# One 512-column matmul for both parts of x in the convolved projection, and a later place for the scan's scaled blocks

## The chip, the cores and the metric

The kernel runs on one core of a Trainium2 chip. The metric is the device time of one execution in microseconds (us); of several runs the median is taken. Five engines work side by side, each in the order of its own queue: TensorE (PE: matmuls; PEld: its weight loads), VectorE (DVE), ScalarE (ACT), GpSimd (POOL) and SyncE (SP), which issues the loads. Tiles in SBUF and accumulators in PSUM (eight banks of 512 float32 columns) pass between them behind semaphores.

## The reference

One layer of a hybrid encoder, 256 tokens (`SEQ`), 2048 features, all float32. What matters here is the first sub-layer:

```python
hn = rmsnorm(h, mix_norm_pre[i])
proj = hn @ w_in[i]                                   # 2048 x 3616
z, xbc, dt_raw, u = jnp.split(proj, split_at, axis=-1)
y_ssd = ssd_mixer(z, xbc, dt_raw, ...)                # below
y_pool = pool_mixer(u, pool_w[i], pool_scale[i])
mix = jnp.concatenate([y_ssd, y_pool], axis=-1) @ w_out[i]
...
def ssd_mixer(z, xbc, dt_raw, conv_w, conv_b, ...):
    xbc = jax.nn.silu(dwconv_centred(xbc, conv_w, conv_b))   # 5 taps along the tokens, 1536 channels
    xs, bm, cm = jnp.split(xbc, [D_SSD, D_SSD + G * SSD_STATE], axis=-1)
    dt = jax.nn.softplus(dt_raw + dt_bias)
    # forward and backward scan in chunks of 128 tokens:
    #   y_diag = (cm bm^T) * decay * dt  @ xs     within a chunk
    #   y_off  = what the other chunk's state adds
    y = (y_fwd + y_bwd + xs * d_skip) * silu(z)
    return group_rmsnorm(y) * norm_w
```

After it come a gated conv-MLP (`w_ffn_up`, `w_ffn_down`) and a gated embedding (`w_ple_gate`, `w_ple`). Their code is not touched.

## The kernel before

Matmuls are made in a rounded float32 format. To keep the accuracy, every operand is split into a high part (rounded by ScalarE, `split` line 152, `put` line 196) and a low part (the rest, VectorE, lines 153 and 197), and a product is the sum of three: high × high, high weights × low x, low weights × high x. Weights arrive by SP in `raw` tiles of 2048 columns (4 buffers) and are split into `whi` and `wlo` tiles of 1024 columns (5 buffers each).

Nothing in the program fixes the order across engines except the order in which it is written (a planner takes what is ready by that order, on times that it estimates, and hands out buffers as they come free) and `issue_after`, which puts an instruction behind another on its engine. The planned order of each engine's queue is then fixed.

The stages at the front, one after another on TensorE: `dtu` (dt and the pool mixer's input, six PSUM buffers), the convolved projection `xbc` in three slabs of 512 features (slab 2, then 0, then 1), and z. PSUM has six `main` buffers of one bank and two `misc` ones.

A slab (`xbc`, line 672) is computed with features on the partitions by `feature_major` (line 300): four units `u`, each of one raw tile (4 blocks of 128 rows of the weights × 512 features), split into two tiles `j`; in a tile two blocks `kk` of rows, each with four blocks `f` of 128 features. For one (`kk`, `f`) the three products are three matmuls of 256 columns (the tokens). `acc` has two main buffers, with two `f` in each. The last unit runs by `f`, so that the first sums are done sooner. `times_rows` (line 426) multiplies the sums from PSUM by the tokens' norm `rxb`, 512 columns at a time. `conv` (line 434) then makes four ScalarE products and 16 VectorE steps, and line 680 finishes the SiLU.

`hn` is a `Panel`: the high parts of x for eight blocks of rows in one page, the low parts in another. `Pairs` (line 180), which the later stage `ga`/`va` uses with `feature_pairs`, keeps high and low parts of a block side by side, so that `both(k)` is one operand of 512 columns; there the sum of the low half is added to the high half at the end by `total` (line 357: a ScalarE copy from PSUM and a VectorE add).

Between units `aside()` runs the next list of jobs in `work`: for the scan `seg` (decays `E`), `cb`, `scale_by_dt` (line 685: eight ScalarE products of a block by dt into a page `w`), `weigh` (line 693: two VectorE operations of 1024 columns on `w` and `E`), `xs_turn`, `far` and `skip` (POOL products), `mix` (the scan's matmuls `yo`, `yd`). The lists stand by slab and by z's eight units (two blocks `k` of 1024 columns each, matmuls of 512 columns in four main buffers).

Of the kernel before, what the change touches and what calls it, by code (L numbers as in the profile page):

```python
# [14 lines left out]
ALU = mybir.AluOpType  # L15

P = 128
L = 256
D = 2048
NK = D // P  # L20
# [31 lines left out]
def build(nc, a, out):  # L52
# [5 lines left out]
    with tile.TileContext(nc) as tc, \  # L58
# [15 lines left out]
        def mid(name, dtype=F32):  # L74
            return gp.tile([P, 1024], dtype, tag="mid", bufs=5, name=name)
# [10 lines left out]
        def mm(o, lhsT, rhs, start, stop):  # L86
            last["pe"] = ins(nc.tensor.matmul(o, lhsT, rhs, start=start, stop=stop, skip_group_check=True))  # L87
# [53 lines left out]
        def parts(name):  # L141

            if name in spare:
                return spare.pop(name)
            return [wp.tile([P, 1088], F32R, tag=tag, bufs=5, name=f"{name}{tag}") for tag in ("whi", "wlo")]

        def split(dst, src, c0, *cuts):

            hi, lo = dst
            for c1 in cuts:  # L150
                s = slice(c0, c1)
                last["act"] = ins(nc.scalar.copy(hi[:, s], src[:, s]))
                last["dve"] = ins(nc.vector.tensor_sub(lo[:, s], src[:, s], hi[:, s].bitcast(F32)))  # L153
                c0 = c1
            return hi, lo
# [144 lines left out]
        def feature_major(name, w, c0, get, acc):  # L300

            for u in range(4):
                r = raw(f"{name}r{u}", w[u * 512:(u + 1) * 512, c0:c0 + 512]
                        .rearrange("(k p) c -> p k c", p=P), 4, 512)
                tiles = []

                def step(j, kk, f):
                    k = 4 * u + 2 * j + kk
                    (wh, wl), (xh, xl) = tiles[j], get(k)
                    s = slice(kk * 512 + f * P, kk * 512 + (f + 1) * P)  # L310
                    for q, (ww, xx) in enumerate(((wh, xh), (wh, xl), (wl, xh))):
                        mm(acc[f // 2][:, f % 2 * L:(f % 2 + 1) * L], ww[:, s], xx,
                           k == 0 and q == 0 and f % 2 == 0, k == NK - 1 and q == 2)

                for j in range(2):
                    tiles.append(split(parts(f"{name}{u}_{j}"), r[:, j * 1024:(j + 1) * 1024], 0, 1024))
                    if u < 3:
                        for kk in range(2):
                            for f in range(4):
                                step(j, kk, f)  # L320
                if u == 3:
                    for f in range(4):
                        for j in range(2):
                            for kk in range(2):
                                step(j, kk, f)
                aside()

        def feature_pairs(name, w, c0, get, acc):
# [27 lines left out]

        def total(o, acc):

            for f in range(2):
                nc.scalar.copy(o[:, f * L:(f + 1) * L], acc[f][:, L:])  # L360
                nc.vector.tensor_add(o[:, f * L:(f + 1) * L], o[:, f * L:(f + 1) * L], acc[f][:, :L])

# [60 lines left out]
            nc.vector.tensor_add(o4[:, :, :L - 1], o4[:, :, :L - 1], b4[:, :, 1:])  # L423
            return o

        def times_rows(name, acc, rb):
            o = mid(name)
            for i in range(2):
                nc.vector.tensor_tensor(o[:, i * 512:(i + 1) * 512].rearrange("p (f t) -> p f t", f=2),
                                        acc[i].rearrange("p (f t) -> p f t", f=2),  # L430
                                        rb.unsqueeze(1).to_broadcast([P, 2, L]), op=ALU.mult)
            return o

        def conv(name, acc, taps, wcol, wstep, bcol):

            cv = mid(name)
# [11 lines left out]
            return cv  # L448


        hn = Panel("hn")

        def x_panel(k0, k1):
            for k in range(k0, k1):
# [215 lines left out]
                nc.scalar.activation(xs[:, t * 1024 + slab * 512:t * 1024 + (slab + 1) * 512], ps, AF.Copy, scale=0.5)  # L670

        def xbc(slab):
            acc = main(f"xbc{slab}")
            feature_major(f"xb{slab}", w_in, DSSD + slab * 512, hn, acc)
            sc = times_rows(f"xr{slab}", acc, rxb)
            cv = conv(f"cv{slab}", sc, 5, V_SCW + 4 * slab, 12, V_SCB + 4 * slab)
            th = mid(f"th{slab}")
            nc.scalar.activation(th, cv, AF.Tanh, scale=0.5)

            nc.vector.scalar_tensor_tensor(cv, th, 1.0, cv, op0=ALU.add, op1=ALU.mult)  # L680
            return cv
# [47 lines left out]
        def job(f, *args):  # L729
# [15 lines left out]
        ])  # L745
        xa = xbc(0)
        work.extend([
            [job(seg, 3), job(scale_by_dt, 0, 0, 0)],
            [job(seg, 4), job(scale_by_dt, 0, 0, 1), job(weigh, 0, 0)],
            [job(seg, 5), job(xs_turn, xa, 0)],  # L750
            [job(seg, 6)],
        ])
# [14 lines left out]
        zacc = [main(f"z{t}") for t in range(2)]  # L767
# [382 lines left out]
```

## Time and profile before

| | |
|---|---|
| median of 3 runs | 1118.17 us (1117.62 to 1120.74) |
| the profiled execution | 1116.37 us, of which the span from first to last instruction 1114.6 |
| granted TensorE clock | 0.998 |
| busy: PE, DVE, ACT, POOL | 1102.6, 834.2, 683.7, 53.0 us |
| matmuls of the three slabs | from 52.4 to about 139.8 us, 576 of them |
| z | from 140.3 to about 195 us |
| DMA queue q1 | 274.33 MB, 73.3% of 16 engines' span |

The page of the profile gives busy times by engine, the chain of work that ended last, and the costliest groups of instructions, each named by the tiles that it writes and reads (`xbc<-hnh,xb_0whi` is a matmul into `xbc` from the high part of x and the high weights of a slab's even tile). In the views that follow, an instruction row is: start, length, engine, line, operation, names, shapes, and in brackets the idle time ahead of it with what ended it. A matmul's row is longer than its share of the pipeline; the pitch from start to start is what it costs. A slab is shown under one name (`xbc`), all its tiles under `xb_0`, `xb_1`.

### The profile page before, as it was taken

How to read it: one execution, taken by the hardware profiler on the slowest of the kernel's cores; microseconds unless marked ns; L12 is line 12 of the kernel's file. 1: busy time of each engine (PE TensorE's matmuls, PEld its weight loads, DVE VectorE, ACT ScalarE, POOL GpSimd, SP SyncE). 2: the span in 40 equal slices, each digit the busy share in tenths (PEclk: the TensorE clock that was granted, in tenths of full speed). 3: DMA queues.
4: the chain of work that ended last, by engine and by line, in shares of the span. 5: the costliest groups of instructions: out<-in, count | busy, mean ns of one | idle time of the engine just before them, and what ended most of it. 6: DMA issues, size and time to landing. Idle time of an engine off the chain costs nothing.

```text
span 1114.6 us, 15714 instructions
## 1 busy us (share of the span) xinstructions
PE 1102.6 (99%) x6040; PEld 964.0 (86%) x6040; DVE 834.2 (75%) x1047; ACT 683.7 (61%) x1006; POOL 53.0 (5%) x80
## 2 busy tenths in 40 slices
PE   9999999999999999999999999999999999999996
PEld 9999988888788888888888888888888888887885
DVE  6668888879786866767767777676888787897574
ACT  6757876555775565565655655556666466657462
POOL 0300023100200000000000000000000000001001
PEclk9999999999999999999999999999999999999999
DMA  9954445766587977877887797676888789886732
GB/s 354 375 175 150 154 151 186 262 215 224 213 283 252 302 264 247 272 268 255 270 296 254 241 323 255 211 254 205 279 293 303 255 285 314 307 283 214 247 132 76
DMA packets 145739, 275.69 MB, mean 247 GB/s; under 512 B 5504, under 2 KB 98560, under 8 KB 142208
## 3 DMA queue, kind: packets, MB, share of 16 engines
q1 hardware_dynamic: 145376, 274.33, 73.3%
q8 instruction: 47, 0.77, 0.3%
q10 hardware_dynamic: 288, 0.36, 0.1%
q14 instruction: 28, 0.23, 0.1%
HBM read 251.86 MB, written 22.81 MB: 246 GB/s over the span
## 4 chain that ended last, share of the span: by engine, by line
PE 92%; DMA 3%; ACT 2%; issue 1%; DVE 1%; POOL 0%; SPq 0%; DVEq 0%; POOLq 0%; ACTq 0%
PE va L87 22%; PE ga L87 21%; PE dna L87 15%; PE gt L87 7%; PE woa L87 7%; PE xbc L87 6%; PE dns L87 5%; PE z L87 4%; DMA dtur<-w_in 2%; DMA x<-x 1%; PE wos L87 1%; PE yd L87 1%; PE pw L87 1%; PE ple L87 0%; PE seg L87 0%
## 5 line engine op out<-in xcount | busy, mean ns | idle before, releaser
L87 PE MATMUL ga<-wox,ug_0whi 128*128 128x512 f32 x352 | 87.8, 391 | 0.0
L87 PE MATMUL va<-wox,uv_0whi 128*128 128x512 f32 x352 | 87.6, 391 | 0.0
L87 PE MATMUL ga<-wox,ug_1whi 128*128 128x512 f32 x352 | 87.2, 389 | 0.0
L87 PE MATMUL va<-wox,uv_1whi 128*128 128x512 f32 x352 | 86.9, 389 | 0.0
L87 PEld LDWEIGHTS va<-wox,uv_1whi 128*128 128x128 f32 x352 | 66.1, 188 | 13.7
L87 PEld LDWEIGHTS ga<-wox,ug_1whi 128*128 128x128 f32 x352 | 66.0, 188 | 13.7
L87 PEld LDWEIGHTS va<-wox,uv_0whi 128*128 128x128 f32 x352 | 64.6, 188 | 12.5
L87 PEld LDWEIGHTS ga<-wox,ug_0whi 128*128 128x128 f32 x352 | 64.6, 188 | 12.4
L87 PE MATMUL ga<-wox,ug_1wlo 128*128 128x256 f32 x352 | 49.7, 283 | 0.9 <-DVE ug_1wlo L153 0.9
L87 PE MATMUL ga<-wox,ug_0wlo 128*128 128x256 f32 x352 | 49.5, 283 | 0.0
L87 PE MATMUL va<-wox,uv_1wlo 128*128 128x256 f32 x352 | 49.4, 283 | 0.0
L87 PE MATMUL va<-wox,uv_0wlo 128*128 128x256 f32 x352 | 49.2, 283 | 0.0
L87 PEld LDWEIGHTS ga<-wox,ug_0wlo 128*128 128x128 f32 x352 | 46.8, 191 | 1.8
L87 PEld LDWEIGHTS va<-wox,uv_0wlo 128*128 128x128 f32 x352 | 46.7, 191 | 1.7
L87 PEld LDWEIGHTS ga<-wox,ug_1wlo 128*128 128x128 f32 x352 | 45.4, 192 | 1.3 <-DVE ug_1wlo L153 1.3
L87 PEld LDWEIGHTS va<-wox,uv_1wlo 128*128 128x128 f32 x352 | 45.4, 192 | 0.0
L875 POOL TENSOR_SCALAR dnm<-dnq,fmean 128x1 f32<-128x1 f32 x2 | 0.6, 282 | 586.8 <-ACT dnj L872 586.8
L87 PE MATMUL xbc<-hnh,xb_0whi 128*128 128x256 f32 x96 | 27.6, 288 | 0.3 <-ACT u L539 0.3
L87 PE MATMUL xbc<-hnh,xb_1whi 128*128 128x256 f32 x96 | 27.3, 285 | 0.0
L87 PE MATMUL xbc<-hnl,xb_1whi 128*128 128x256 f32 x96 | 27.2, 283 | 0.0
L87 PE MATMUL xbc<-hnh,xb_1wlo 128*128 128x256 f32 x96 | 27.1, 283 | 0.0
L87 PE MATMUL xbc<-hnh,xb_0wlo 128*128 128x256 f32 x96 | 27.1, 283 | 0.0
(1664 smaller groups left out, 3095.6 us busy)
## 6 DMA issues: line engine op xcount, KB each, us to landing
dn0r<-w_ffn_down SPq DMA_DIRECT2D x15, 1024.0 KB, 6.2
dn1r<-w_ffn_down SPq DMA_DIRECT2D x15, 1024.0 KB, 6.9
br<-w_ffn_down SPq DMA_DIRECT2D x14, 1024.0 KB, 5.5
bm<-block SPq DMA_DIRECT2D x14, 1024.0 KB, 5.0
zr<-w_in SPq DMA_DIRECT2D x8, 1024.0 KB, 5.3
wo0r<-w_out SPq DMA_DIRECT2D x8, 1024.0 KB, 5.8
gt0r<-w_ple_gate SPq DMA_DIRECT2D x8, 1024.0 KB, 5.9
gt1r<-w_ple_gate SPq DMA_DIRECT2D x8, 1024.0 KB, 5.5
```

The source lines that it names most:

```text
L87: last["pe"] = ins(nc.tensor.matmul(o, lhsT, rhs, start=start, stop=stop, skip_group_check=True))
L875: nc.gpsimd.tensor_scalar(m, q, 1.0 / D, mean[t], op0=ALU.mult, op1=ALU.add)
```

## The change

Three things are done together. First, `hn` becomes `Pairs`, and `feature_major` makes of the first two of the three products one matmul of 512 columns (high weights × both parts of x) into a bank of its own, the third a 256-column matmul into that bank's second half; a slab has four main buffers (`xbc` and `xbd`). Second, the order in a unit: both tiles are split first; in units 1 and 2 all 16 high or all 16 low matmuls run together (unit 1 low first, unit 2 high first); units 0 and 3 go by `f`, four high and four low matmuls for each. The sums are then made by `total` (four copies and four adds of 256 columns) and one multiplication by `rxb` over 1024 columns. Third, `scale_by_dt` and `weigh` leave slab 1 and stand a unit or two later in z's list.

```diff
             for u in range(4):
                 r = raw(f"{name}r{u}", ...)
-                tiles = []
-                def step(j, kk, f):
...
-                    for q, (ww, xx) in enumerate(((wh, xh), (wh, xl), (wl, xh))):
-                        mm(acc[f // 2][:, f % 2 * L:(f % 2 + 1) * L], ww[:, s], xx,
-                           k == 0 and q == 0 and f % 2 == 0, k == NK - 1 and q == 2)
...
+                r = r[:, :1024], r[:, 1024:]
+                tiles = [split(parts(f"{name}{u}_{j}"), r[j], 0, 1024) for j in range(2)]
+
+                def step(low, j, kk, f):
                     k = 4 * u + 2 * j + kk
+                    ww = tiles[j][low][:, kk * 512 + f * P:kk * 512 + (f + 1) * P]
+                    if low:
+                        mm(acc[f][:, L:], ww, get(k)[0], False, False)
+                    else:
+                        mm(acc[f], ww, get.both(k), k == 0, False)
+
+                steps = [(j, kk, f) for j in range(2) for kk in range(2) for f in range(4)]
+                if u in (0, 3):
+                    steps.sort(key=lambda x: x[2])
+                n = 4 if u in (0, 3) else 16
+                for q in range(0, 16, n):
+                    for low in (1, 0) if u and (u + q // 4) % 2 else (0, 1):
+                        for x in steps[q:q + n]:
+                            step(low, *x)
                 aside()
...
-        hn = Panel("hn")
+        hn = Pairs("hn")
...
         def xbc(slab):
-            acc = main(f"xbc{slab}")
+            acc = main(f"xbc{slab}") + main(f"xbd{slab}")
             feature_major(f"xb{slab}", w_in, DSSD + slab * 512, hn, acc)
-            sc = times_rows(f"xr{slab}", acc, rxb)
+            sc = mid(f"xr{slab}")
+            total(sc, acc)
+            s4 = sc.rearrange("p (f t) -> p f t", f=4)
+            nc.vector.tensor_tensor(s4, s4, rxb.unsqueeze(1).to_broadcast([P, 4, L]), op=ALU.mult)
...
-            [job(seg, 3), job(scale_by_dt, 0, 0, 0)],
-            [job(seg, 4), job(scale_by_dt, 0, 0, 1), job(weigh, 0, 0)],
+            [job(seg, 3)],
+            [job(seg, 4)],
             [job(seg, 5), job(xs_turn, xa, 0)],
             [job(seg, 6)],
...
-            [job(seg, 7), job(scale_by_dt, 0, 1, 0)],
-            [job(scale_by_dt, 0, 1, 1), job(weigh, 0, 1)],
-            [job(xs_turn, xb, 1), job(far, 1), job(skip, 0), job(scale_by_dt, 1, 0, 0)],
-            [job(far, 0), job(skip, 1), job(scale_by_dt, 1, 0, 1), job(weigh, 1, 0)],
-            [job(mix, 0, 0), job(scale_by_dt, 1, 1, 0)],
-            [job(mix, 0, 1), job(scale_by_dt, 1, 1, 1), job(weigh, 1, 1)],
-            [job(mix, 1, 0)],
+            [job(seg, 7)],
+            [job(scale_by_dt, 0, 0, 0), job(scale_by_dt, 0, 0, 1)],
+            [job(xs_turn, xb, 1), job(far, 1), job(skip, 0), job(weigh, 0, 0), job(scale_by_dt, 0, 1, 0)],
+            [job(scale_by_dt, 0, 1, 1), job(weigh, 0, 1), job(far, 0), job(skip, 1), job(scale_by_dt, 1, 0, 0)],
+            [job(mix, 0, 0), job(scale_by_dt, 1, 0, 1), job(weigh, 1, 0)],
+            [job(mix, 0, 1), job(scale_by_dt, 1, 1, 0), job(scale_by_dt, 1, 1, 1)],
+            [job(mix, 1, 0), job(weigh, 1, 1)],
             [job(mix, 1, 1)],
```

`total` now runs over all buffers that it is given (`len(acc)`) and `times_rows` is gone.

More of the change, by code (lines that the diff above doesn't have):

```diff
@@ L304, in feature_major @@
                         .rearrange("(k p) c -> p k c", p=P), 4, 512)
-                tiles = []
-                def step(j, kk, f):
+                r = r[:, :1024], r[:, 1024:]
+                tiles = [split(parts(f"{name}{u}_{j}"), r[j], 0, 1024) for j in range(2)]
+                def step(low, j, kk, f):
                     k = 4 * u + 2 * j + kk
-                    (wh, wl), (xh, xl) = tiles[j], get(k)
-                    s = slice(kk * 512 + f * P, kk * 512 + (f + 1) * P)
-                    for q, (ww, xx) in enumerate(((wh, xh), (wh, xl), (wl, xh))):
-                        mm(acc[f // 2][:, f % 2 * L:(f % 2 + 1) * L], ww[:, s], xx,
-                           k == 0 and q == 0 and f % 2 == 0, k == NK - 1 and q == 2)
[L315 to L325, printed above, removed]
+                    ww = tiles[j][low][:, kk * 512 + f * P:kk * 512 + (f + 1) * P]
[11 more added lines that the diff above has]
+                            step(low, *x)
                 aside()
@@ L357, in total @@
         def total(o, acc):
-            for f in range(2):
+            for f in range(len(acc)):
                 nc.scalar.copy(o[:, f * L:(f + 1) * L], acc[f][:, L:])
@@ L424, in taps @@
             return o
[L426 to L432, printed above, removed]
         def conv(name, acc, taps, wcol, wstep, bcol):
```

## Prediction

> **What bounds the kernel now.** I read the page first, its busy times and its chain, then the chain of waits piece by piece over the stage that changes, then who waited for whom there, then the time lines of VectorE and ScalarE.
>
> ```profile
> span 1114.6 us, 15714 instructions
> PE 1102.6 (99%) x6040; PEld 964.0 (86%) x6040; DVE 834.2 (75%) x1047; ACT 683.7 (61%) x1006; POOL 53.0 (5%) x80
> PE 92%; DMA 3%; ACT 2%; issue 1%; DVE 1%; POOL 0%; SPq 0%; DVEq 0%; POOLq 0%; ACTq 0%
> ...
> PE xbc L87 <- ACT u L539: 0.3, 1, 0.3
> ```
>
> The last row is the only wait that the view of waits gives for PE from 48 to 200 us, which holds the whole changed stage: the three slabs of the convolved projection (in the order 2, 0, 1) and z. TensorE is the bound there. A microsecond taken from its stream is a microsecond of the kernel, as long as no new wait opens; other engines matter through the leads that they have on it.
>
> **The matmuls.** All 576 matmuls of the projection have 256 columns. These are pieces of the chain of waits (start, length, what; the last slab ends where the `seg` row begins, and the `yd` row is used further down):
>
> ```profile
> 93.79 5.76 PE xbc L87 x48
> 120.36 5.74 PE xbc L87 x48
> 139.81 0.47 PE seg L87 x2
> 140.28 5.45 PE z L87 x24
> 193.42 1.73 PE yd L87 x16
> 338.31 22.23 PE ga L87 x128
> ```
>
> 48 narrow ones take 5.74 to 5.76 us: 119.7 ns each, 359 ns for the three of one block. The later stage `ga` already does what the change does here (one 512-column matmul for both parts of x, one of 256 for the low weights): 128 in 22.23 us, 347.3 ns a pair. z's 24 matmuls of 512 columns give 227 ns each, and 347 − 120 agrees. After the change the 192 blocks have 384 matmuls: 192 × (359 − 347) = 2.3 us saved (2.2 to 2.4 with the two readings of a unit), all on the path.
>
> The Trainium skill, "TensorE: Matmul & The Clock Gate", section "Back-to-back issue gap", gives a warm gap of N/2.4 + 2.5 ns. By that rule the block falls from 327.5 to 325 ns, an estimate of 0.5 us in all. The trace does not agree: 119.7 and 227 ns carry some 13 ns above N/2.4, so the measured saving is the larger one.
>
> **The start.** The first slab takes the buffers of the `dtu` sums; its second buffer came late:
>
> ```profile
> 52.41 0.36 PE L87 MATMUL xbc<-hnh,xb_0whi 128*128 128x256 f32 x1
> 53.09 0.28 PE L87 MATMUL xbc<-hnh,xb_0wlo 128*128 128x256 f32 x1
> 53.69 0.39 PE L87 MATMUL xbc<-hnh,xb_0whi 128*128 128x256 f32 x1 [0.32 <-ACT u L539]
> 53.11 0.53 ACT L539 ACTIVATE u<-dtu,rx0r 128x320 f32<-128x320 f32 x1 [1.65 <-DVE dt L538]
> 54.89 0.55 ACT L542 ACTIVATE u<-dtu,rx1r 128x352 f32<-128x352 f32 x1
> 51.69 1.22 DVE L153 TENSOR_TENSOR xb_1wlo<-xb2r,xb_1whi 128x1024 fp32r<-128x1024 f32 x1
> ```
>
> From 53.09 to 53.69 is 0.6 us where 0.12 is the pitch: 0.48 us lost. The new order does all of f = 0 first (8 matmuls, 4 × 347 = 1.39 us), so the second buffer is wanted at 53.8, after the 53.64 at which ScalarE is done; the third and fourth at 55.2 and 56.6, against 55.44 for the last of the `dtu` evictions. It asks for the second low tile at 53.5, ready at 52.91. So 0.5 us more is gained, with 0 as the other end.
>
> **What is added.** Leaving PSUM was one multiplication per two blocks; now it is copy, add, multiply.
>
> ```profile
> L360 ACT COPY gr<-ga x44: 372/378/382, 308.0 to 760.7; 128x256 f32<-128x256 f32 x44
> L361 DVE TENSOR_TENSOR gr<-gr,ga x44: 411/414/416, 308.8 to 761.5; 128x256 f32<-128x256 f32 x44
> L429 DVE TENSOR_TENSOR xr<-xbc,rxb x6: 682/688/693, 79.4 to 140.1; 128x512 f32<-128x512 f32 x6
> L680 DVE SCALAR_TENSOR_TENSOR cv<-th,cv x3: 1206/1215/1217, 97.0 to 150.1; 128x1024 f32<-128x1024 f32 x3
> L690 ACT ACTIVATE w<-cbm,dt x64: 385/390/405, 110.3 to 173.4; 128x128 f32<-128x128 f32 x64
> L696 DVE TENSOR_TENSOR w<-w x4: 1208/1217/1882, 122.0 to 174.9; 128x1024 f32<-128x1024 f32 x4
> L698 DVE TENSOR_TENSOR E<-E,w x4: 1206/1214/1225, 123.5 to 177.2; 128x1024 f32<-128x1024 f32 x4
> L446 DVE SCALAR_TENSOR_TENSOR cv<-xr,vt,cv x48: 465/476/484, 86.1 to 147.9; 128x254 f32<-128x254 f32 x24, 128x255 f32<-128x255 f32 x24
> ```
>
> Per slab ScalarE gets four copies (1.5 us) and VectorE four adds and a 1024-wide multiply, priced by the row of that width (4 × 0.414 + 1.215), less two at 0.688: +1.5 us. Nothing goes to POOL or SP. On the path this costs nothing as long as the weight tiles still come ahead of TensorE. The work is hidden by this slack:
>
> ```profile
> 86.00:106.00 20.00, 20.00 (x165) 19.87 (x165) 20.00 (x34) 14.58 (x23) 0.00 (x0) 1.00 0.37 115
> 113.00:126.00 13.00, 13.00 (x107) 12.82 (x106) 12.93 (x24) 12.14 (x23) 0.00 (x0) 1.00 0.25 83
> 140.00:153.00 13.00, 13.00 (x60) 10.74 (x59) 13.00 (x22) 11.71 (x21) 0.00 (x0) 1.00 0.25 81
> 153.00:166.00 13.00, 13.00 (x61) 10.76 (x61) 8.27 (x8) 7.58 (x15) 6.43 (x3) 1.00 0.69 244
> ```
>
> Columns: length, then busy time of PE, PEld, DVE, ACT, POOL, the clock (1.00 throughout), DMA. VectorE is full from 86 to 106, from 113 to 126 and from 140 to 153, and free by a third after. That is where the moves bear: weighing (0,0) and (0,1) began at 122.0 and 146.8 (a row of the next fence), 2 × 2.4 us, and now stand behind z's units 2 and 3, past 153; the scaled blocks before them (8 × 0.39 = 3.1 us of ScalarE a set, less where they overlap) go the same way. Neither issues a DMA, and none of SP's loads is moved past another; on ScalarE they go behind the casts of z's tiles, on POOL nothing of theirs runs. From 86 to 153 VectorE gets some 3 us (slabs 0 and 1) and gives up 4.8.
>
> **The leads.** In units 1 and 3 the new order starts with low weights and walks through both tiles at once, so the second low tile is wanted 0.96 us after unit 1 begins (8 narrow matmuls) rather than after a whole tile (24, 2.9 us).
>
> ```profile
> 92.78 1.22 DVE L153 TENSOR_TENSOR xb_1wlo<-xb0r,xb_1whi 128x1024 fp32r<-128x1024 f32 x1
> 119.49 1.21 DVE L153 TENSOR_TENSOR xb_1wlo<-xb1r,xb_1whi 128x1024 fp32r<-128x1024 f32 x1
> 123.29 0.28 PE L87 MATMUL xbc<-hnh,xb_1wlo 128*128 128x256 f32 x1
> 115.55 4.02 DVE L446 SCALAR_TENSOR_TENSOR cv<-xr,vt,cv 128x254 f32<-128x254 f32 x10
> 146.80 1.22 DVE L696 TENSOR_TENSOR w<-w 128x1024 f32<-128x1024 f32 x1
> 151.20 1.22 DVE L153 TENSOR_TENSOR z_0wlo<-zr,z_0whi 128x1024 fp32r<-128x1024 f32 x1
> 152.51 0.71 PE L87 MATMUL z<-z_0wlo,hnh 128*128 128x512 f32 x2
> ```
>
> Slab 1, unit 1: ready at 120.70, used at 123.29, lead 2.6. The unit's two first tiles of matmuls begin near 120.2; the new use would be 121.2 less the 2.3 us by which TensorE is then early, some 118.9. Left in place the tile would be 1.8 us late. It need not stay: it sat behind ten convolution steps (0.40 us apart), and the convolution now starts later, as its input is one multiply over the finished slab, while the tile's slot is free when the last slab's f = 3 ends its high pass, about 1 us before that slab's end. VectorE, waiting for copies and sums, has room for it. I take no stall; the other end is 1.8. Slab 0, unit 1: ready 94.00, new use about 92.2 + 1.0 = 93.2: late 0.8 if it stays, the same reason for 0.
>
> z, fifth tile: ready 152.42, used 152.51, lead 0.1. TensorE is there 2.8 us earlier. From the slab's end VectorE has now: add, multiply, 16 convolution steps, two minima, one low tile, gate product, then this tile: 0.4 + 1.1 + 6.4 + 1.2 + 1.1 + 1.1 + 1.2 = 12.5 us against the 12.7 that TensorE takes from the slab's end (139.8) to that use. Before, the two weighing steps (2.3) stood there and four convolution steps and the first multiply were already past. So it is a draw; I take 0.3 us lost, between 0 and 2.
>
> Four of the six main buffers are now one slab's. The next slab's f = 2 needs one of them 2.8 us after it starts, and f = 0 of the old slab ended 4.2 us before its end (three more blocks of 1.39): room of about 7 us for a copy, an add and their waits (1.3 us). Only behind slab 2 is ScalarE not free:
>
> ```profile
> 84.33 0.72 ACT L598 ACTIVATE seg_w<-seg_c,small 32x512 fp32r<-32x512 f32 x1
> L597 ACT ACTIVATE seg_x<-seg_c,small x4: 722/722/724, 79.2 to 83.6; 32x512 fp32r<-32x512 f32 x4
> 82.27 2.88 PE pw L87 x24
> 188.68 0.69 ACT L785 ACTIVATE zt<-z,rz 128x512 f32<-128x512 f32 x1 [2.80 <-PE z L87]
> ```
>
> With the four of line 598 between, the last of which is the first row, it is taken from 79.2 to 85.1. `pw` stands between the slabs (2.9 us), so the first freed buffer is wanted near 86.7 in the new time, after 85.1 − 1.1 + 0.9: cost 0, other end 0.5. z wants its third buffer 1.4 us in and has two free, so slab 1's first sums must be out by then: 4 us of room.
>
> The later moves: weighing (1,1) goes from z's unit 5 to 6 behind the first three mixes, whose POOL adds it does not feed; its reader is the last `yd`, at 193.42 now, and VectorE had ended it by 178.4 (line 698, last start 177.2). One unit is about 8 us: still 6 before. The page of its scaled blocks is held as long; the next page wanted is `zt`, at 188.7. The far blocks' POOL products keep their place; weighings now run beside them (one row of 1.88 instead of 1.22 us shows that price), in a stretch a third free. `hn` kept in pairs changes addresses: 0.
>
> **The sum.** 2.3 + 0.5 − 0.3 = 2.5 us. The profiled execution took 1116.37 us (span 1114.6) and becomes 1113.9; the median shown, 1118.17, stands 1.8 above it and becomes 1115.7. A measurement of this kernel tells about 0.3%, 3.4 us, from no change, so the forecast is a true gain inside that bound.
>
> **Rivals.**
> 1. *Low tiles late.* One or two of the three tight places keep their place in VectorE's queue: 0.8 to 2 us each, 1117 to 1118.5. For it: the full stretches, and that a queue in order lets the tile wait behind the convolution. Against: the weighings gone, and slots free earlier.
> 2. *Slower: the convolution in front.* If the low tile of unit 1 stands behind the whole later convolution (multiply done about 2.5 us after the slab's end, 16 steps of 0.40, a minimum, the tile 1.2), it is ready 10.7 us after the end, where unit 1's second low tile is wanted at 0.5 + 5.6 + 0.5 + 1.0 = 7.5 in slab 1: 3.2 us; in slab 0, with `seg_x` in the way of the copies, about as much. 6.4 − 2.8 = +3.6: 1121.8. It decides from 1.4 us of waiting per slab on. Against: the tile of slab 1 stood behind a run of ten steps, not all 16, and the multiply leaves VectorE idle just when the tile can be made.
> 3. *Sums hold the banks.* The start or slab 0 waits for buffers: 0.5 to 1 (the other ends above), so 1116.5. The Trainium skill, "Trainium Kernel Development and Optimization", section "Best Practices", warns of this side: faster matmuls don't speed up the emptying of PSUM. The 7 us of room behind each sum speak against it here.
> 4. *More than the pitch.* No tile is late (2.8 gained), and the median of the new runs lies nearer to its profiled execution than the 1.8 us of before (the fastest of the three, 1117.62, is 0.6 under the median): 3.4 or more, 1114.3.
> 5. *The pitch doesn't fall.* A wide matmul costs here what two narrow ones did, 240 ns, and only the start is gained: 1118.17 − 0.5 = 1117.7. z's 227 ns and the 347 of `ga` speak against it. The formula cited above from "TensorE: Matmul & The Clock Gate" of the Trainium skill would come near to this one.
>
> **Chances.** Forecast 0.50, rival 1 0.17, rival 2 0.07, rival 3 0.06, rival 4 0.15, rival 5 0.05. Faster by over 0.3% (below 1114.8): rival 4 and a sixth of the forecast, 0.23. Slower (above 1121.5): most of rival 2, 0.06. Within: 0.71. The range goes from 1113.7, a little under rival 4, to 1118.6, the end of rival 1; rival 2 and the outer tails are left out.
>
> **What would show it.** Units of the projection with 32 matmuls in 16 × 347 ns = 5.56 us; no wait of PE for `u` at 53 us; z beginning near 137.5 instead of 140.28; PE waits from 48 to 200 us under 0.5 us; no weighing before 150. Wrong would be: PE rows waiting for `xb_1wlo` or `z_0wlo` of line 153, or for the add of the sums; units of the projection still near 5.75; or a gain at z's start that is gone by the last `yd`.

## The result, and the profile after

Slower by 0.34%: 1122.15 us median (1121.2 to 1123.92, 7 runs) against 1118.17 (1116.46 to 1120.74, 7 runs), ratio 1.0034, 95% interval 1.0021 to 1.0046. The forecast was 1115.7 in a range that ended at 1118.6. The profiled execution took 1121.25 us.

The head of the page of the profile after (span; busy times):

```profile
span 1119.5 us, 15354 instructions
PE 1102.8 (99%) x5848; PEld 952.7 (85%) x5848; DVE 836.0 (75%) x1056; ACT 688.0 (61%) x1018; POOL 51.3 (5%) x80
```

192 matmuls fewer, and TensorE's busy time is what it was: 0.2 us more. Something took the gain back. The view of waits for PE from 48 to 200 us, which had one row of 0.3 us before, names it (waited for; total, times, longest):

```profile
PE z L87 <- DVE z_1wlo L153: 1.4, 1, 1.4
PE z L87 <- ACT z_1whi L152: 1.3, 1, 1.3
PE z L87 <- DVE z_0wlo L153: 0.6, 2, 0.5
PE yd L87 <- DVE y L720: 0.4, 1, 0.4
PE seg L87 <- DVE catl L197: 0.3, 1, 0.3
```

The stall is in z; in the slabs there is one short wait, `seg` for `catl` in slab 0. z goes through 16 blocks of rows, k0 to k15, two in each of its units; an odd block's tiles are `z_1whi` and `z_1wlo`. By the starts of TensorE's first matmul of each stage (the column "last `yd`" by the last), after less before:

| slab 2 | z's first | k6 to k10 | k11 | k12 | last `yd` | `ga` | end |
|---|---|---|---|---|---|---|---|
| +0.61 | −1.98 | −1.20 | +0.27 | +2.86 | +3.22 | +3.85 | +4.88 |

The whole projection gained 2.6 us (from +0.61 to −1.98; the 0.61 at the front isn't the change's, since another execution of this kernel, r2 below, shows 0.00 there). z lost 5.2, of it 4.1 from k10 to k12, the stage behind z 0.6, and the stage `dn` 1.1.

The gain, from the chain of after: 32 matmuls of the first unit of slab 1 take 2.79 + 2.81 = 5.60 us, where 48 took 5.74 to 5.76 in other units before.

```profile
113.08 2.79 PE xbc L87 x16
115.87 2.81 PE xbd L87 x16
```

The loss, from VectorE's time line, first before (start, length, what, and in brackets the idle time ahead and its releaser):

```profile
162.59 1.83 DVE L153 TENSOR_TENSOR xd<-xd,xd 128x1024 fp32r<-128x1024 f32 x1 [2.88 <-ACT xd L152]
165.88 1.39 DVE L153 TENSOR_TENSOR xd<-xd,xd 128x1024 fp32r<-128x1024 f32 x1 [1.46 <-ACT xd L152]
168.23 1.88 DVE L696 TENSOR_TENSOR w<-w 128x1024 f32<-128x1024 f32 x1 [0.96 <-ACT w L690]
171.29 0.68 DVE L720 TENSOR_TENSOR ym<-yo,dec 128x512 f32<-128x512 f32 x1
171.90 1.21 DVE L153 TENSOR_TENSOR z_1wlo<-zr,z_1whi 128x1024 fp32r<-128x1024 f32 x1
174.29 0.69 DVE L727 TENSOR_TENSOR y<-y,yd 128x512 f32<-128x512 f32 x1 [1.18 <-POOL y L722]
```

And after:

```profile
162.94 1.83 DVE L153 TENSOR_TENSOR xd<-xd,xd 128x1024 fp32r<-128x1024 f32 x1 [2.88 <-ACT xd L152]
167.64 1.84 DVE L689 TENSOR_TENSOR w<-w 128x1024 f32<-128x1024 f32 x1 [2.87 <-ACT w L683]
169.40 1.21 DVE L153 TENSOR_TENSOR xd<-xd,xd 128x1024 fp32r<-128x1024 f32 x1
...
171.67 0.68 DVE L713 TENSOR_TENSOR ym<-yo,dec 128x512 f32<-128x512 f32 x1
173.80 0.69 DVE L720 TENSOR_TENSOR y<-y,yd 128x512 f32<-128x512 f32 x1 [1.45 <-POOL y L715]
174.40 1.22 DVE L689 TENSOR_TENSOR w<-w 128x1024 f32<-128x1024 f32 x1
175.54 1.22 DVE L153 TENSOR_TENSOR z_1wlo<-zr,z_1whi 128x1024 fp32r<-128x1024 f32 x1
```

`z_1wlo` is the low tile of k11. Before, it stood ahead of `y<-y,yd` and was made at 171.90. After, it stands behind a weighing that waits 2.87 us for ScalarE's products, behind a sum that waits 1.45 us for POOL, and behind one more weighing: made at 175.54. Between its rows VectorE stands idle for 2.88, 2.87 and 1.45 us, and nothing from further back in its queue is taken forward into that time. The tile's own input, the high tile, came at 174.18 (ScalarE's rows below), so both queues make it late. The Trainium skill, "TensorE: Matmul & The Clock Gate", in the table ahead of "What a matmul computes", calls the queues of ScalarE, VectorE and GpSimd strict first-in first-out; these rows agree.

ScalarE's time line for the high tile of the same block, before and then after:

```profile
162.46 2.45 ACT L690 ACTIVATE w<-cbm,dt 128x128 f32<-128x128 f32 x8
165.76 4.78 ACT L690 ACTIVATE w<-cbm,dt 128x128 f32<-128x128 f32 x16
170.45 1.03 ACT L152 CAST z_1whi<-zr 128x1024 fp32r<-128x1024 f32 x1
```

```profile
161.86 1.05 ACT L152 CAST xd<-xd 128x1024 fp32r<-128x1024 f32 x1 [3.85 <-POOL xd L698]
162.81 4.79 ACT L683 ACTIVATE w<-cbm,dt 128x128 f32<-128x128 f32 x16
167.51 1.03 ACT L152 CAST xd<-xd 128x1024 fp32r<-128x1024 f32 x1
168.44 4.79 ACT L683 ACTIVATE w<-cbm,dt 128x128 f32<-128x128 f32 x16
173.15 1.03 ACT L152 CAST z_1whi<-zr 128x1024 fp32r<-128x1024 f32 x1
```

32 products now stand between the first far block's cast (`xd`) and k11's; before there were 24, and k11's cast began at 170.45. TensorE's time line shows where it took the low tile before, without a wait, and both waits after (the second bracket is the low tile):

```profile
174.41 0.62 PE L87 MATMUL z<-z_1wlo,hnh 128*128 128x512 f32 x2
174.23 1.20 PE L87 MATMUL z<-z_1whi,hn 128*128 128x512 f32 x4 [1.31 <-ACT z_1whi L152]
176.81 0.73 PE L87 MATMUL z<-z_1wlo,hn 128*128 128x512 f32 x2 [1.39 <-DVE z_1wlo L153]
```

From start to start the two waits cost 3.0 us of pitch, and the wait of `yd` for `y` a little later 0.6. Before, the low tile was ready at 173.11 and used at 174.41: a lead of 1.3 us.

### The profile page after: what moved, and what is told of

Its sections match the earlier page's. It is cut to its first block, busy times and chain, and to the rows that moved or that the text cites. A ratio compares the mean times of both kernels' runs of the same rounds, so it can differ in the third digit from the quotient of the medians.

```text
span 1119.5 us, 15354 instructions
## 1 busy us (share of the span) xinstructions
PE 1102.8 (99%) x5848; PEld 952.7 (85%) x5848; DVE 836.0 (75%) x1056; ACT 688.0 (61%) x1018; POOL 51.3 (5%) x80
## 4 chain that ended last, share of the span: by engine, by line
PE 84%; DVE 6%; ACT 4%; DMA 2%; POOL 2%; issue 1%; POOLq 0%; SPq 0%; DVEq 0%; ACTq 0%
PE va L87 22%; PE ga L87 21%; PE dna L87 13%; PE gt L87 7%; PE woa L87 5%; PE dns L87 4%; PE dtu L87 4%; PE xbc L87 2%; PE xbd L87 2%; DMA sums<-sums 1%; DVE cv L436 1%; PE z L87 1%; DMA dtur<-w_in 1%; ACT w L683 1%; PE wos L87 1%
## 5 line engine op out<-in xcount | busy, mean ns | idle before, releaser
L979 ACT ACTIVATE fc<-fc 128x1024 f32<-128x1024 f32 x11 | 11.7, 1062 | 24.9 <-DVE fc L421 24.9
L418 ACT ACTIVATE fc<-gr,vt 128x256 f32<-128x256 f32 x44 | 25.9, 588 | 0.0
L87 PE MATMUL dna<-dn_0wlo,hidh 128*128 128x512 f32 x76 | 24.2, 389 | 0.0
L87 PE MATMUL dna<-dn_1wlo,hidh 128*128 128x512 f32 x76 | 24.2, 389 | 0.0
L87 PE MATMUL dna<-dn_0whi,hidl 128*128 128x512 f32 x76 | 24.2, 389 | 0.0
```

The source lines that it names most:

```text
L418: nc.scalar.activation(o[:, c], x[:, c], AF.Identity, bias=vec(bcol + f), scale=vec(wcol + NF + f))
L979: nc.scalar.activation(cv, cv, AF.Gelu_apprx_tanh)
```

## The experiments

Two theories at first. *Order*: the moved jobs carry waits of their own, and z's tiles k10 to k12 stand behind them in VectorE's and ScalarE's queues. *Matmuls*: the new projection itself (its sums, pages or order) spoils something. Within order, a narrower one: ScalarE's products alone are what delays. Ratios are against the kernel before on the same chip; where an interval stands, 6 to 12 runs of the kernel and 19 to 33 of before. "Lists" are the job lists by slab and unit.

### The two halves of the change apart

**e1_matmul_only**: the new matmuls and sums, the lists of before.

```diff
-            [job(seg, 3)],
-            [job(seg, 4)],
+            [job(seg, 3), job(scale_by_dt, 0, 0, 0)],
+            [job(seg, 4), job(scale_by_dt, 0, 0, 1), job(weigh, 0, 0)],
...                                  # and z's lists as before
```

> The changed matmuls, sums and unit order, with the job lists of the kernel before (scaled blocks and weighings in their old places). Jobs theory (the later scaled blocks queue up on ScalarE in front of the casts of z's tiles k11 and k12, which TensorE then waits for): the 4 us lost between z's k10 and k13 do not occur; z still starts about 2 us earlier, the tile k4 may lose up to 2 us since a weighing is back in front of it; total 1116 to 1119 us. Sums theory (the copies, adds and the later convolution push VectorE and ScalarE work into z): z still loses 4 us or more, total 1121 to 1123.

Measured: 1119.72 us, ratio 1.0015 (1.0006 to 1.0023). z begins 2.6 us earlier, there is no wait at k11, and one at k4, the fifth tile, which stands behind both halves of weighing (0,1) and the whole later convolution (view of waits):

```profile
PE z L87 <- DVE z_0wlo L153: 1.8, 1, 1.8
```

z ends 0.5 us earlier; `dn` then takes 2.3 us more in the profiled execution. The jobs theory's mechanism holds (nothing is lost from k10 to k13); its total of at most 1119 is missed by 0.7. This run can't show what k11 would do to a larger lead, since k4 had already taken 2.1 us of it.

**e2_jobs_only**: the kernel before with the changed lists and nothing else.

```diff
-            [job(seg, 3), job(scale_by_dt, 0, 0, 0)],
-            [job(seg, 4), job(scale_by_dt, 0, 0, 1), job(weigh, 0, 0)],
+            [job(seg, 3)],
+            [job(seg, 4)],
...                                  # and z's lists as changed
```

> The kernel before with the changed job lists alone; matmuls and sums as before. Jobs theory: waits of TensorE in z for the tiles k11 and k12 behind long runs of ScalarE products, 3 to 4 us lost, total 1121 to 1122.5. Sums theory: no new wait, 1117.5 to 1119.

Measured: 1122.45 us, ratio 1.0041 (1.0028 to 1.0054): the lists alone, on the old matmuls, cost as much as the whole change. The same tile stands in the same place (VectorE's time line, then the view of waits):

```profile
173.32 0.69 DVE L727 TENSOR_TENSOR y<-y,yd 128x512 f32<-128x512 f32 x1 [1.48 <-POOL y L722]
173.93 1.22 DVE L696 TENSOR_TENSOR w<-w 128x1024 f32<-128x1024 f32 x1
175.06 1.22 DVE L153 TENSOR_TENSOR z_1wlo<-zr,z_1whi 128x1024 fp32r<-128x1024 f32 x1
PE z L87 <- DVE z_1wlo L153: 1.3, 1, 1.3
```

z ends 2.7 us later, and 0.6 more go behind it; `dn` is unchanged. In after z ends only 0.5 us later than here, though its projection was faster: the low tile of k11 is ready at about the same time (176.28 here, 176.76 in after), and what TensorE had gained ahead of it is waited away. The second theory is not needed for the loss in z.

**e3_pairs_only**: the kernel before with `hn` kept in pairs.

```diff
-        hn = Panel("hn")
+        hn = Pairs("hn")
```

> The kernel before with hn kept in pairs of pages alone. In the changed kernel the first matmul of the projection came 0.6 us later than before, already in the dtu stage. If the pairs layout (or the queue order that is planned from it) causes that, it is here too: first slab 0.6 us later, total 1118.5 to 1119; if not, 1118.2 and the slab at 52.4 us.

Measured: 1117.37 us, ratio 0.9997 (0.9988 to 1.0005). Nothing up to `dn`, so the 0.6 us at the front of after isn't the layout's; in `dn` +0.6 in the profiled execution.

### Which of the moved jobs

**e4_scaled_early**: the change, the scaled blocks back in their old places, the weighings late.

```diff
-            [job(seg, 3)],
-            [job(seg, 4)],
+            [job(seg, 3), job(scale_by_dt, 0, 0, 0)],
+            [job(seg, 4), job(scale_by_dt, 0, 0, 1)],
...
-            [job(scale_by_dt, 0, 0, 0), job(scale_by_dt, 0, 0, 1)],
+            [job(scale_by_dt, 0, 1, 1)],
...                                  # weigh(0,0) in z's unit 2, (0,1) in 3, (1,0) in 4
```

> The changed kernel with the scaled blocks back in the places of the kernel before and the weighings left at their later places. If the ScalarE products are what holds z (jobs theory, ScalarE half), the waits at k11 and k12 go and k4 keeps the relief of VectorE: 1115.5 to 1117.5. If the later weighings on VectorE hold z, it stays at 1121 to 1122.

Measured: 1118.23 us, ratio 0.9998 (0.9988 to 1.0008). z is 2.1 us ahead until k11, loses 1.2 to k12 (wait for `z_1wlo` 0.9), and ends 0.9 ahead; `dn` +2.8. The total lies between the two forecasts. Up to k11 both queues have the order of the kernel before again (24 products ahead of the cast; VectorE's low tile between `ym` and `y`, at 172.14 against 171.90):

```profile
172.14 1.21 DVE L153 TENSOR_TENSOR z_1wlo<-zr,z_1whi 128x1024 fp32r<-128x1024 f32 x1
```

So the weighings' later place is not what is left. The tile is nearly as early as before, and TensorE comes 2.1 us sooner to a tile that had a lead of 1.3. What stands ahead of it did not move forward with TensorE: POOL's first far product ends at 161.47 before, 161.73 here and 161.82 in after (the last section shows why).

**e5_scaled_before_far**: the change, the second direction's first products ahead of the far blocks.

```diff
-            [job(xs_turn, xb, 1), job(far, 1), job(skip, 0), job(weigh, 0, 0), job(scale_by_dt, 0, 1, 0)],
-            [job(scale_by_dt, 0, 1, 1), job(weigh, 0, 1), job(far, 0), job(skip, 1), job(scale_by_dt, 1, 0, 0)],
+            [job(xs_turn, xb, 1), job(scale_by_dt, 1, 0, 0), job(far, 1), job(skip, 0), job(weigh, 0, 0)],
+            [job(scale_by_dt, 1, 0, 1), job(weigh, 0, 1), job(far, 0), job(skip, 1)],
...                                  # the other sets in their old places, as in e4
```

> The kernel of e4 (changed matmuls, scaled blocks in their old places, weighings late) with the scaled blocks (1,0) written ahead of the far products in z's units 2 and 3, so that ScalarE makes them while it waits for POOL and not between the cast of the far product and that of z's tile k11. In e4 z is 2.1 us ahead up to k11 and 0.9 after it. ScalarE-queue theory: the cast of k11 comes 2 to 4 us sooner, no wait at k11 and k12, z's last matmuls 2 us ahead of the kernel before; total 1116 to 1117. If VectorE's late weighings hold k11 and not ScalarE, z stays 0.9 ahead: 1117.5 to 1118.5.

Measured: 1120.07 us, ratio 1.0023 (1.0009 to 1.0037): a miss. The stall moved to k10, whose low tile fell behind the splits of the far blocks and a weighing beside POOL's products (VectorE's time line, then the view of waits):

```profile
162.54 4.67 DVE L153 TENSOR_TENSOR xd<-xd,xd 128x1024 fp32r<-128x1024 f32 x2 [2.89 <-ACT xd L152]
167.14 2.92 DVE L691 TENSOR_TENSOR E<-E,w 128x1024 f32<-128x1024 f32 x1
169.98 1.21 DVE L153 TENSOR_TENSOR z_0wlo<-zr,z_0whi 128x1024 fp32r<-128x1024 f32 x1
PE z L87 <- DVE z_0wlo L153: 1.9, 1, 1.9
```

**e6_wide_products**: the change, half of the sets of eight products made as two of four times the width.

```diff
         def scale_by_dt(d, g, t):
+            if t:
+                for h in (0, 4):
+                    nc.scalar.activation(ww[t, g][:, ...four heads...], cbm[:, d, g, t, :].unsqueeze(1)
+                                         .to_broadcast([P, 4, P]), AF.Copy, scale=dt[...head h...])
+                return
```

> The changed kernel with each of the four scaled sets of the second token tile made by two 512-column ScalarE instructions in place of eight of 128 (they take the first head's dt for four heads: that part of the computation is changed, sizes and order stay). A set falls from 2.4 to about 1.1 us, 5 us of ScalarE less in z's units 3 to 5. ScalarE-queue theory: the waits for k11 and k12 (3 us) go, z ends 1 us ahead of the kernel before: total 1117 to 1118.5. Rival (POOL's far products and VectorE set the time there): 1120.5 to 1122.

Measured: 1122.48 us, ratio 1.0037 (1.0023 to 1.0051): a miss, above both ranges, and it decides. ScalarE's cast of k11 comes 2.8 us sooner than in after, VectorE's low tile 0.3 us later (time lines of ScalarE and VectorE, then the view of waits):

```profile
170.37 1.04 ACT L152 CAST z_1whi<-zr 128x1024 fp32r<-128x1024 f32 x1
175.24 0.69 DVE L727 TENSOR_TENSOR y<-y,yd 128x512 f32<-128x512 f32 x1 [1.17 <-POOL y L722]
175.84 1.22 DVE L153 TENSOR_TENSOR z_1wlo<-zr,z_1whi 128x1024 fp32r<-128x1024 f32 x1
PE z L87 <- DVE z_1wlo L153: 3.6, 1, 3.6
```

"ScalarE's products alone" falls: the high tile is there at 171.41, the low one is begun 4.4 us later. What holds k11 here is its place behind the sum that waits for POOL. The planner also changed VectorE's order with the shorter products (a second weighing now stands ahead of that sum), so the run does not price the products by themselves.

**r1_before_again** and **r2_after_again**: both kernels once more.

> The kernel before once more, for a second profile. In the profiles so far the kernels with the changed matmuls lost 1.1 to 2.8 us in the down projection (dna/dns), whose queues are the same in all kernels. If that is scatter of the executions, the stage's length (224.9 us from first to last dna matmul before) will differ here by a microsecond or more; if it belongs to the changed kernels, it is 224.9 again.

> The changed kernel once more, for a second profile. Scatter: the down projection takes another time than 225.95 us; property of the kernel: 225.9 again. The waits of z at k11 and k12 (3 us) and at k4 (0.6 us) must be there again, and the dtu stage shows whether its 0.6 us belongs to the kernel.

Measured: before 1116.51 us, every stage within 0.2 us of its first profile. After 1124.67, with the same two waits at k11 (1.3 and 1.4) and 0.6 at k4, and then a third loss: TensorE's clock. The view by stretches (length; busy time of PE, PEld, DVE, ACT, POOL; granted clock; DMA) for r2, and two rows of its TensorE:

```profile
175.00:190.00 15.00, 13.79 (x64) 11.56 (x65) 8.80 (x10) 8.98 (x18) 4.19 (x2) 0.77 0.32 95
177.22 1.05 PE L87 MATMUL z<-z_1whi,hn 128*128 128x512 f32 x2
178.08 1.05 PE L87 MATMUL z<-z_1wlo,hn 128*128 128x512 f32 x2
```

Two matmuls take 0.86 us here, 0.46 in the first profile (from 177.39 to 177.85), where the clock of that stretch was 1.00. From k11 to k12 that is 2.7 us more, of the kernel's two profiles in this one alone; e5 and e6 show 0.89 there.

### Putting the order right

**e8_fewer_ahead**: the new matmuls; the jobs where the low tile of k11 no longer stands behind a sum of the mix.

```diff
-            [job(seg, 3)],
-            [job(seg, 4)],
+            [job(seg, 3), job(scale_by_dt, 0, 0, 0)],
+            [job(seg, 4), job(scale_by_dt, 0, 0, 1), job(weigh, 0, 0)],
...
+            [job(seg, 7), job(scale_by_dt, 0, 1, 0)],
+            [job(scale_by_dt, 0, 1, 1)],
+            [job(weigh, 0, 1), job(xs_turn, xb, 1), job(far, 1), job(skip, 0), job(scale_by_dt, 1, 0, 0)],
+            [job(far, 0), job(skip, 1), job(scale_by_dt, 1, 0, 1)],
+            [job(mix, 0, 0)],
+            [job(weigh, 1, 0), job(mix, 0, 1), job(scale_by_dt, 1, 1, 0), job(scale_by_dt, 1, 1, 1)],
             [job(mix, 1, 0), job(weigh, 1, 1)],
```

> The changed matmuls with new lists: sets of the first token tile in their old places, weighing (0,1) at the head of z's unit 2, the sets (1,1) and weighing (1,0) behind the tile k11. In the planned queues the low tile of k11 now stands right behind the far products' splits and one weighing step, and 16 products, not 32, stand ahead of its cast. Order theory (what costs is the place of z's tiles k10 to k12 in the fixed queues of VectorE and ScalarE behind jobs that themselves wait for POOL and for the mix): no wait over 0.5 us in z, z's end 2 us or more ahead of the kernel before, total 1115.5 to 1117.5. Load theory (too much work for VectorE in that stretch whatever its order): 1119 or more.

Measured: 1116.68 us against 1117.27, ratio 0.9990 (0.9981 to 0.9999), the fastest of all by the ratio. The tile stands ahead of the sums again (VectorE's time line), and no weight tile is in the view of waits:

```profile
168.06 1.88 DVE L689 TENSOR_TENSOR w<-w 128x1024 f32<-128x1024 f32 x1 [0.97 <-ACT w L683]
169.86 1.21 DVE L153 TENSOR_TENSOR z_1wlo<-zr,z_1whi 128x1024 fp32r<-128x1024 f32 x1
```

z is 2.8 us ahead at k11 and 2.0 at its end; 0.9 go at the next stage, where TensorE waits 0.7 for `catl` (line 197). Of the whole time 0.1% is left as a gain.

**e10_tiles_first**: the change with its own lists; in z the split of the next unit's tiles is written ahead of the jobs.

```diff
-                    two = ready.pop(name) if u == 0 and name in ready else split_two(name, w, k0, c0)
+                    two = ready.pop(name) if name in ready and (u == 0 or name == "z") else split_two(name, w, k0, c0)
...
                 group = []
+                if name == "z" and u + 1 < nu:
+                    ready[name] = split_two(name, w, ks[2 * u + 2], c0)
                 aside()
```

> The changed kernel with its own lists; only in z the split of the next unit's two tiles is written ahead of the jobs of a unit, so that the planner gives z's tiles precedence over jobs. The low tile of k11 then stands before the first sum of the mix in VectorE's queue, and 8 products fewer stand ahead of its cast. Order theory: of the 3 us at k11 at least 1.5 go, 1118.5 to 1120.5; load theory: 1121.5 to 1122.5.

Measured: 1117.84 us, ratio 1.0003 (0.9994 to 1.0012). The low tile of k11 stands ahead of `y` and of a weighing step again (VectorE's time line), and 24 products, not 32, ahead of its cast:

```profile
171.48 1.21 DVE L153 TENSOR_TENSOR z_1wlo<-zr,z_1whi 128x1024 fp32r<-128x1024 f32 x1
```

z loses 0.9 us from its first matmul to its last `yd` where after lost 5.2: 4.3 us by the place in the queues alone, with every job in the unit that the change gave it. VectorE's wait of 2.87 us for the products is still there; it doesn't cost when the tile isn't late by it. z ends 1.5 us ahead of before. Then 1.8 us of waiting for `catl`.

**e11_both** (e8's lists and e10's split) and **e12_old_matmuls** (the same two on the old matmuls):

> The lists of e8 and the tiles first, as in e10. Order theory: TensorE waits nowhere in z, the whole 2.6 us of the matmuls reach z's end: 1115 to 1117. Load theory: 1119 or more.

> The kernel before (three matmuls of 256, its sums) with the lists and the precedence of e11. It had no wait in z that these could take away, so no gain: 1117.5 to 1119. The difference to e11 is then what the changed matmuls and sums are worth where nothing holds z: 2.3 to 2.8 us. If e12 gains as well, the lists do it.

Measured: 1117.53 us, ratio 1.0003 (0.9994 to 1.0012), z's end 1.1 ahead (a wait of 1.0 for the sum `y` comes up); and 1117.34, ratio 0.9999 (0.9990 to 1.0008), 0.2 us ahead from start to end. Better order alone gives nothing on the old matmuls, whose tiles were on time. But e11 was to lie 2.3 to 2.8 us below e12, and the medians are equal within 0.2: in z's end 0.9 us of the new matmuls' 2.4 are left, and in the whole time nothing that can be told from the scatter.

### What `dn` takes back

In every profile with the new matmuls the stage `dn`, 600 us later and with the same queues in the same order, is longer. Three more runs:

> The kernel before with hn kept as Pairs and nothing else, as in e3_pairs_only, in a second execution. Every kernel with the changed matmuls lost 0.2 to 2.8 us in the stage dn; from its first to its last matmul it took 224.85 to 224.87 us with the old matmuls and a Panel (four executions), 225.51 us in e3, 225.1 to 227.7 us with the changed matmuls. Theory (the addresses of the pages, which Pairs shift, disturb that stage): again 225.3 us or more, span 1115.1. Rival (scatter from execution to execution): 224.9, span 1114.6, or another value that has nothing to do with e3's.

> The kernel of e8_fewer_ahead in a second execution; its dn took 226.37 us. If the length of dn belongs to a kernel, 226.3 to 226.4 us and a span of 1114.9; if it scatters from execution to execution, another value between 225.0 and 227.7, and the span with it. z's part should come out as in e8 in both cases: no wait of TensorE above 0.4 us for a weight tile from 48 to 200 us.

> e8_fewer_ahead with each 512-column matmul of the convolved projection made as two of 256 columns into the same two halves of the same bank: banks, order, sums, Pairs and lists as in e8, the number of TensorE instructions and the pitch as before (576 matmuls). The 2.3 us of the wide matmul go away: z begins 2.3 us later than in e8, about at 140.0 to 140.5. For dn: if fewer TensorE instructions ahead of it are what disturbs it (the stream's 192 missing matmuls shift how it is fetched), 224.9 us; if the layout of hn or the sums, 225.3 us or more; if it scatters, any value from 224.9 to 227.7.

```diff
-                        mm(acc[f], ww, get.both(k), k == 0, False)
+                        mm(acc[f][:, :L], ww, get(k)[0], k == 0, False)
+                        mm(acc[f][:, L:], ww, get(k)[1], False, False)
```

From the first to the last matmul of `dna`, in us:

| | executions | us |
|---|---|---|
| `hn` a Panel: before, r1, e2, e12 | 4 | 224.85 to 224.87 |
| Pairs alone: e3, e13 | 2 | 225.51, 226.25 |
| one kernel twice: e8, e14 | 2 | 226.37, 224.98 |
| 192 matmuls put back: e15 | 1 | 226.73 |
| all with Pairs | 13 | 224.98 to 227.70, median 226.03 |

The number of instructions isn't it (e15), nor is it a fixed cost of a kernel (e8 and e14 are one kernel). With Pairs the length scatters from execution to execution; with the Panel it did not in four. But four are few, and these four are at the fast end: e2's other timed runs took 1.8 to 4.7 us more than its profiled one, and the kernel before, with the Panel, ran from 1116.06 to 1119.58 us in the 33 runs beside e8 (e8, with Pairs, from 1116.04 to 1117.74 in 11). So it isn't shown that the Panel is free of this, nor that Pairs cause it.

The lost time lies in another place each time (near 958 us in after, 931 and 942 in e8, 874 to 877 in e13, 999 in e3). In e8 and e13 the chain of waits leads back to transfers: in e8 from 941.85 to the load `sums`, 6.7 us from issue to landing (median 5.9 in this stage), in e13 from 876.75 to a load `dn0r` of `w_ffn_down`, 8.2 us (the median of the largest is 7.2). The view by stretches shows e8 and then e14 from 900 to 960 us: TensorE idle for 0.76 us, then full, with a DMA share of 0.84 and 0.88.

```profile
900.00:960.00 60.00, 59.24 (x260) 48.20 (x259) 49.73 (x53) 37.97 (x44) 0.00 (x0) 1.00 0.84 292
900.00:960.00 60.00, 60.00 (x267) 49.67 (x266) 51.67 (x55) 38.42 (x44) 0.00 (x0) 1.00 0.88 308
```

Why these transfers took longer stays open, and where the other executions lost theirs is not shown. Over e3's 11 timed runs the layout costs at most 0.6 us (the interval's end).

e15 also prices the wide matmul by itself: z's second block starts at 142.92, in e8 and e14 at 140.13 and 140.40. With the 0.1 and 0.4 us by which e15's projection began earlier, that is 2.9 us; of it 0.3 comes from the wait of `seg` for `catl` in slab 0, which is longer in e15 (0.53 us idle, 0.27 in after).

## Why the prediction was wrong

- **The pitch: right.** Two gains of 2.3 and 0.5 were summed to z's start; 2.6 came in after and 2.4 in e1 and e8. The wide matmul gave more than its 2.3, 2.9 by e15, and the new order and sums took 0.4 where 0.5 was to come: with narrow matmuls (e15) z's second block is 0.07 us later than before although the projection began 0.37 earlier. That the total came out near 2.8 is in part luck.
- **The start: right in kind.** No kernel with the new order waits for `u` near 53 us. The first unit took 6.16 to 6.56 us in six executions with the old order and 6.04 in e15, so it gave 0.1 to 0.5, where the forecast was 0.5 with 0 as the other end.
- **The low tiles of the slabs, the banks: right at 0.** No wait for `xb_1wlo` or for a sum; the one new wait in the slabs, `seg` for `catl`, is 0.3 us. Of rival 1's three places the two in the slabs did not stall, the fifth tile of z did. Rival 2's 1121.8 is near the result by luck, since its place did not stall (its 0.5 + 5.6 + 0.5 + 1.0 also gives 7.6, not 7.5).
- **The fifth tile of z: 0.3 forecast, 0 to 2 as ends.** After lost 0.8 there, e1 2.1, e4 and e8 nothing.
- **The later moves: the step that failed.** The prediction's sum has no term for the moved weighings and products, since they run "in a stretch a third free", from a row with VectorE busy 8.27 of 13.00 us. That row was read as room. The idle time there was VectorE waiting, 2.88 us for the cast behind POOL's product and 1.46 for the next, with later instructions standing behind. The moved jobs did not fill these gaps. They put 8 more products ahead of the cast of k11, and its low tile behind a sum that waits for POOL and a weighing step. Cost 4.4 us (z's 5.2 less the fifth tile's 0.8) instead of 0. Shown by e2 (the lists alone, on the old matmuls, end z 2.7 later, although TensorE comes to k11 1.2 us later than in after and the tile had 1.3 of lead), e10 (4.3 come back by order alone) and e8.
- **A tight place that the prediction did not list: k11.** Its low tile had a lead of 1.3 us before, less than the 2.5 to 2.8 by which TensorE was to come earlier. With the old order kept it would have cost about a microsecond by itself: 1.2 in e4, where nothing else holds it.
- The prediction did count ScalarE's share ("behind the casts of z's tiles"), with the sign wrong: at k11 the products stand ahead of the cast, 32 of them.
- **"hn kept in pairs changes addresses: 0".** Up to `dn` yes; in `dn` the profiles with Pairs lose 0.1 to 2.8 us, in e8 and e13 behind transfers that took longer, by a cause that stays open.
- **The sum.** −2.0 at z's start, +5.2 in z, +0.6 behind it, +1.1 in `dn`: +4.9, the difference of the spans. The prediction's own sign of being wrong, a gain at z's start that is gone by the last `yd`, is what happened.

## What to carry to other kernels

On engines with fixed queues a busy share is no measure of room. Before a job is moved, list for the next tile that the bound engine needs what will stand ahead of it on each engine, which of those instructions wait for somebody else, and how much lead the tile has; if the bound engine becomes faster, that lead shrinks wherever the work ahead of the tile doesn't come forward with it. A job that waits on POOL or on a chain of small products can cost its wait, not only its length. Where the order is by program order, write the tiles ahead of the jobs. And time the parts of a joint change apart: here the matmuls brought 2.6 us up to z, and the lists alone cost 4.6 (e2's ratio). The parts don't add up: a stall swallows the gain that comes ahead of it.

## What the runs showed of the hardware

- Two waits of TensorE of 1.3 and 1.4 us, 1.2 us of matmuls apart, were followed by matmuls at about half speed in r2 (granted clock 0.77 from 175 to 190 us) and not in the first profile of the same kernel (1.00). The same stretch shows 0.89 in e5 (waits of 1.9 and 1.0 us) and e6 (one of 3.6), and 1.00 in e1 (no wait from 165 to 190 us) and e4 (one of 0.9). The Trainium skill, "TensorE: Matmul & The Clock Gate", section "HAM oscillation — how this bites in real kernels", has as the rule no idle gap over about 3.4 us; each gap of r2 was under half of that. That the waits lowered the clock is likely, but not shown: the same two waits went with it in one execution of two.
- VectorE and POOL hold each other up on products and splits of 1024 columns. POOL's two far products took 3.77 us before, and 5.55 after, where VectorE split z's tiles beside the first of them; VectorE's 1024-column product of 1.21 us took 2.92 in e5, beside POOL. POOL's time line, before and after:

```profile
159.57 3.77 POOL L705 TENSOR_TENSOR xd<-xs,dec 128x1024 f32<-128x1024 f32 x2 [82.54 <-ACT xs L670]
158.14 5.55 POOL L698 TENSOR_TENSOR xd<-xs,dec 128x1024 f32<-128x1024 f32 x2 [82.17 <-ACT xs L660]
```

The Trainium skill, "SBUF — State Buffer", section "SBUF: two separate sides", says that a VectorE instruction with two SBUF inputs and a GpSimd instruction that reads SBUF can't use a shared port pair together: whichever starts first holds it for its whole length. The traces agree: in the 17 profiles all 46 VectorE instructions between 158 and 171 us that took over 1.3 us began beside a POOL product and ended 1.08 to 1.09 us after it (in before 164.43 after 163.34, in e5 170.06 after 168.97), about the length of such an instruction alone, 1.21.

The traces show one thing more: POOL did not get its turn between VectorE instructions that follow each other without a gap, though VectorE did between two POOL products (in e5 the split that ends at 164.37 comes between products of POOL that end at 163.28 and 166.13). In all 17 profiles the first far product ends 1.76 or 1.77 us after the end of the last VectorE instruction beside it, whether it began 0.1 us before that end (before, 1.91 long) or 3.0 (e8, 4.75 long, with three splits beside it). So a far product that is released earlier ends no earlier while VectorE has tiles to split: with the new matmuls it began 0.2 to 3.0 us earlier than before and ended from 0.4 earlier to 2.1 later. With it the work ahead of k11's tile stayed where it was, although TensorE came sooner.
